# Feed-forward input projections by seven quarter products in place of eight, weights prepared from a work list, output projection in six stretches

## The chip, the cores and the metric

The kernel runs on 1 core of one Trainium2 chip. The metric is the device time of one execution in microseconds (us). Before the change the median of three runs is 1221.57 us (1219.39, 1221.57 and 1223.93). The profile comes from one execution of its own, which took 1222.08 us.

## The reference

The program computes one transformer block on 512 tokens of width 1024, in float32: a norm with modulation, one wide input projection, two attention-like branches (stick-breaking attention and retention), their output projections with gates, and then a gated feed-forward. The change touches the end of it, with `w_out` 1024x1024, `w_ffn_in` 1024x5632 and `w_ffn_out` 2816x1024:

```python
        merged = (g_sb * jnp.einsum('bse,ed->bsd', o_sb, w_proj_sb[l])
                  + g_ret * jnp.einsum('bse,ed->bsd', o_ret, w_proj_ret[l]))
        x = x + gate1[:, None, :] * jnp.einsum('bsd,de->bse', merged, w_out[l])

        hffn = modulate(rmsnorm(x, g_norm2[l]), shift2, scale2)
        a, u = jnp.split(jnp.einsum('bsd,df->bsf', hffn, w_ffn_in[l]), 2, axis=-1)
        x = x + gate2[:, None, :] * jnp.einsum('bsf,fd->bsd', jax.nn.silu(a) * u, w_ffn_out[l])

    return rmsnorm(x, g_final)
```

## The kernel before

**Numbers in two parts.** Activations are kept transposed, feature on the 128 partitions and the 512 tokens on the free axis. Every float32 operand is split in two: a high part, which ACT writes as a rounded copy (`fp32r`, L203), and a low part, which DVE writes as source minus high part (L205). A product of two such pairs is three matmuls (`mm3`): high by high, high by low, low by high. The low by low part is left out. `weight` loads one 128x1024 block of weights (512 KB, by a DMA that SP issues at L198 into one of three `raw` buffers), and splits it into one of three `whi` and three `wlo` buffers; `gemm` runs `mm3` over the blocks of the contraction. All matmuls of the kernel are issued at one line, L224.

**The stages from `w_out` on.** The output projection (`wo`) makes eight column blocks of 128. Each has 24 matmuls over all 512 tokens, and `residual`, one DVE operation that multiplies by the gate and adds to `x1`. `add_residual` treats the last three (NSPLIT) differently: it runs them over the first 256 tokens, then over the second, so that the norm of the first half (`half_rms`: column sums by small matmuls in a PSUM tile `z`, a reciprocal square root, a broadcast by small matmuls) is worked on beside the matmuls of the second. `norm2` then scales and splits 256 tokens of each of the eight activations (`xn`, L908 and L909, then L203 and L205) into `hf`, tiles of tag `q`.

The feed-forward has 22 column blocks of 128, each with a weight block for `a` and one for `u` (24 matmuls each, 512 wide, into PSUM tiles `ps`). `ff_act` then makes silu(a) times u: ACT's silu from PSUM (L917), DVE's product (L918), and a split. The blocks run in three chunks of 8, 8 and 6 (`FF_CHUNKS`). After each chunk its part of `w_ffn_out` is multiplied, eight output blocks, each added to `x1` at L951; the last chunk does this through `add_residual` again, followed by the final norm and the stores.

**The order.** The program is written in the order in which it should run, and the tile framework gives each instruction its place on its engine by that order and by when buffers come free; a tile of a tag waits for the last reader of the tile that had its buffer. Each engine takes its instructions in order and waits at semaphores. In the rows of orders further on, "waits Activation_49" is a wait for ACT, DVE_49 for DVE, PE_49 for PE, DMAHW for a transfer that SP issued, DMASW for one that POOL issued; numbers behind names tell buffers apart.

Of the kernel before, what the change touches and what calls it, by code (L numbers as in the profile page):

```python
# [11 lines left out]
F32 = mybir.dt.float32  # L12
# [7 lines left out]
P = 128  # L20
# [16 lines left out]

PE_SHIFT = (1, 2, 4)

FF_CHUNKS = ((0, 8), (8, 8), (16, 6))  # L40


def weight_plan():
# [38 lines left out]
    for i in range(NF):  # L82
        add(("fa", i), "w_ffn_in", 0, 8, rng(i * P, P))
        add(("fu", i), "w_ffn_in", 0, 8, rng(DFF + i * P, P))
    for c, (k0, nk) in enumerate(FF_CHUNKS):
        for i in range(8):
            add(("fo", c, i), "w_ffn_out", k0 * P, nk, rng(i * P, P))
# [25 lines left out]
def kernel(  # L113
# [20 lines left out]
    def nm(s):  # L134
        uid[0] += 1
        return f"{s}_{uid[0]}"
# [7 lines left out]
    def psz():  # L144
        return pspool.tile([P, S], F32, tag="z", bufs=BUFS["z"], name=nm("z"))

# [76 lines left out]
    def mm(o, lhs, rhs, start, stop):  # L223
        nc.tensor.matmul(o, lhs, rhs, start=start, stop=stop, skip_group_check=True)  # L224
# [6 lines left out]
    def gemm(o, w, acts, start=True, stop=True, t0=0, t1=S):  # L231

        hi, lo = w
        n = len(acts)
        for k in range(n):
            a = acts[k]
            mm3(o, hi[:, k, :], lo[:, k, :], a[:, 0, t0:t1], a[:, 1, t0:t1],
                start and k == 0, stop and k == n - 1)


# [612 lines left out]

    HALVES = (slice(0, 256), slice(256, 512))

    def half_rms(sq, half):
        o = psz()
        for b in range(2):
            c = half.start + b * P
            mm(o[:, b : b + 1], sq[:, c : c + P], ones[:, 0:1], b == 0, b == 1)  # L860
        v = small(4)[:, 0:2]
        nc.vector.tensor_scalar(v, o[:, 0:2], 1.0 / D, EPS, op0=ALU.mult, op1=ALU.add)
        y, cst = rsqrt_act(v)
        r = psz()
        for b in range(2):
            dg = cpool.tile([P, P], F32, tag="diag", bufs=3, name=nm("diag"))
            nc.vector.tensor_scalar(dg, ident, y[:, b : b + 1], cst, op0=ALU.mult, op1=ALU.mult)
            mm(r[:, b * P : (b + 1) * P], ones, dg, b == 0, b == 1)
        return r[:, 0:256]

    x1 = [None] * 8
    NSPLIT = 3

    def add_residual(get, gcol, acc, on_half):


        for d in range(8 - NSPLIT):
            o = ps()
            gemm(o, *get(d))
            nc.vector.scalar_tensor_tensor(  # L880
                x1[d], o, mod[:, gcol + d : gcol + d + 1], x1[d], op0=ALU.mult, op1=ALU.add
            )
            acc = sumsq(x1[d], acc)
        last = [(d, ps(), get(d)) for d in range(8 - NSPLIT, 8)]
        rs = []
        for hv in HALVES:
            for d, o, (w, acts) in last:
                gemm(o[:, hv], w, acts, t0=hv.start, t1=hv.stop)
                nc.vector.scalar_tensor_tensor(
                    x1[d][:, hv], o[:, hv], mod[:, gcol + d : gcol + d + 1], x1[d][:, hv],  # L890
                    op0=ALU.mult, op1=ALU.add,
                )
# [6 lines left out]
        x1[d] = otile()  # L899
        nc.sync.dma_start(x1[d], xT[d * P : (d + 1) * P, :])  # L900

    hf = [pair("q") for _ in range(8)]

    def norm2(n, hv, r):
        for j in range(8):
            a, sh = gains2[j]
            xn = apool.tile([P, 256], F32, tag="v", bufs=BUFS["v"], name=nm("xn"))
            nc.vector.tensor_mul(xn, x1[j][:, hv], r)  # L908
            nc.scalar.activation(xn, xn, AF.Identity, bias=sh, scale=a)  # L909
            split(hf[j][:, 0, hv], hf[j][:, 1, hv], xn)  # L910

    add_residual(lambda d: (weight(("wo", d)), ms), 16, None, norm2)


    def ff_act(a, u, tag):
        t = tmp()
        nc.scalar.activation(t, a, AF.Silu)  # L917
        nc.vector.tensor_mul(t, t, u)  # L918
        hl = pair(tag)
        split(hl[:, 0, :], hl[:, 1, :], t)  # L920
        return hl

    def final_norm(n, hv, r):
        for d in range(8):
# [3 lines left out]
            )  # L928
            nc.sync.dma_start(out[d * P : (d + 1) * P, hv], x1[d][:, hv])

    for c, (k0, nk) in enumerate(FF_CHUNKS):
        acts = []
        tag = "h" if c == 1 else "s"
        for i in range(k0, k0 + nk):
            a, u = ps(), ps()
            wa, wu = weight(("fa", i)), weight(("fu", i))
            if i == 0:
                for hv in HALVES:
                    for o, w in ((a, wa), (u, wu)):
                        gemm(o[:, hv], w, hf, t0=hv.start, t1=hv.stop)  # L940
            else:
                gemm(a, wa, hf)
                gemm(u, wu, hf)
            acts.append(ff_act(a, u, tag))
        if c == 2:
            ln_exp_tables()
        if c < 2:
            for d in range(8):
                o = ps()
                gemm(o, weight(("fo", c, d)), acts)  # L950
                nc.vector.scalar_tensor_tensor(  # L951
                    x1[d], o, mod[:, 40 + d : 41 + d], x1[d], op0=ALU.mult, op1=ALU.add
                )
        else:
            add_residual(lambda d: (weight(("fo", 2, d)), acts), 40, None, final_norm)


def host_constants():
# [63 lines left out]
```

## Time and the profile before

| | us | |
|---|---|---|
| median of three runs | 1221.57 | 1219.39 to 1223.93 |
| profiled execution | 1222.08 | its span, first to last instruction, is 1220.3 |
| PE (matmuls) | 1195.5 | 98% of the span, 5966 matmuls |
| PEld (weight loads, beside PE) | 1010.4 | 83% |
| DVE | 707.9 | 58% |
| ACT | 491.2 | 40% |
| POOL | 12.4 | 1% |
| from the first matmul of `wo` to the first of the feed-forward | 61.62 | 796.28 to 857.90 |
| the feed-forward, up to the last three output blocks' second half | 335.94 | 857.90 to 1193.84 |
| the last half outputs, and the final norm and stores | 14.44 and 12.02 | 1193.84 to 1220.30 |

The granted clock of PE over the execution is 0.997 of full speed. Busy times of matmuls are modelled at their ends and overlap, so the pace of a run of matmuls is read from starts and not from the mean of a group. In a row of a group of instructions stand the line, engine, operation, output and inputs by name, sizes, count, then busy time and the mean of one in ns, then the idle time before them and what ended it. In a row of the timeline the first number is the start and the second the length, both in us from the start of the span.

### The profile page before, as it was taken

How to read it: one execution, taken by the hardware profiler on the slowest of the kernel's cores; microseconds unless marked ns; L12 is line 12 of the kernel's file. 1: busy time of each engine (PE TensorE's matmuls, PEld its weight loads, DVE VectorE, ACT ScalarE, POOL GpSimd, SP SyncE). 2: the span in 40 equal slices, each digit the busy share in tenths (PEclk: the TensorE clock that was granted, in tenths of full speed). 3: DMA queues.
4: the chain of work that ended last, by engine and by line, in shares of the span. 5: the costliest groups of instructions: out<-in, count | busy, mean ns of one | idle time of the engine just before them, and what ended most of it. 6: DMA issues, size and time to landing. Idle time of an engine off the chain costs nothing.

```text
span 1220.3 us, 15168 instructions
## 1 busy us (share of the span) xinstructions
PE 1195.5 (98%) x5966; PEld 1010.4 (83%) x5966; DVE 707.9 (58%) x1139; ACT 491.2 (40%) x765; POOL 12.4 (1%) x36
## 2 busy tenths in 40 slices
PE   8999999999999999999999999999999999999996
PEld 6888778888888888898888888888888888888886
DVE  6888885645554543387878787547433333333335
ACT  5442323322332332376777677325432122322332
POOL 0010000000000000000000000000000000000000
PEclk9999999999999999999999999999999999999998
DMA  9746761231232264426362625332323233233222
GB/s 357 252 128 227 247 227 52 88 103 52 88 111 70 73 171 140 143 73 163 88 153 79 164 66 195 120 104 70 101 89 104 88 102 104 87 104 90 91 78 69
DMA packets 48233, 149.83 MB, mean 123 GB/s; under 512 B 6049, under 2 KB 8225, under 8 KB 48162
## 3 DMA queue, kind: packets, MB, share of 16 engines
q1 hardware_dynamic: 48162, 148.87, 39.1%
q8 instruction: 47, 0.77, 0.3%
q14 instruction: 24, 0.20, 0.1%
HBM read 129.97 MB, written 4.19 MB: 110 GB/s over the span
## 4 chain that ended last, share of the span: by engine, by line
PE 90%; DVE 5%; DMA 3%; ACT 1%; issue 1%; POOL 0%; SPq 0%; DVEq 0%; ACTq 0%
PE ps L224 76%; PE z L224 11%; PE av L224 3%; DMA araw<-wada 3%; DVE araw L251 1%; DVE wlo L205 0%; DVE t L271 0%; DMA o<-xT 0%; DVE o L925 0%; ACT xn L909 0%; DVE s L205 0%; DVE t L644 0%; POOL s L561 0%; DVE t L643 0%; DVE q L205 0%
## 5 line engine op out<-in xcount | busy, mean ns | idle before, releaser
L203 ACT ACTIVATE whi<-raw 128x1024 fp32r<-128x1024 f32 (+1 forms) x182 | 191.1, 1050 | 513.3 <-PE ps L224 415.9
L224 PE MATMUL ps<-h,whi 128*128 128x512 f32 (+1 forms) x1312 | 397.0, 383 | 0.1
L205 DVE TENSOR_TENSOR wlo<-raw,whi 128x1024 fp32r<-128x1024 f32 (+1 forms) x182 | 220.4, 1211 | 172.4 <-ACT whi L203 170.3
L224 PEld LDWEIGHTS ps<-h,whi 128*128 128x128 f32 x1312 | 241.1, 188 | 44.1
L224 PE MATMUL ps<-h,wlo 128*128 128x512 f32 (+1 forms) x656 | 248.3, 382 | 0.0
L224 PE MATMUL ps<-q,whi 128*128 128x512 f32 (+1 forms) x800 | 238.3, 381 | 0.4 <-ACT q L203 0.4
L224 PEld LDWEIGHTS ps<-q,whi 128*128 128x128 f32 x800 | 148.1, 188 | 29.0 <-ACT q L203 0.6
L224 PE MATMUL ps<-s,whi 128*128 128x512 f32 (+1 forms) x580 | 169.9, 376 | 1.5 <-DVE v L205 1.5
L224 PE MATMUL ps<-q,wlo 128*128 128x512 f32 (+1 forms) x400 | 152.3, 381 | 2.1 <-DVE wlo L205 2.1
L224 PEld LDWEIGHTS ps<-h,wlo 128*128 128x128 f32 x656 | 123.4, 188 | 23.2
L224 PEld LDWEIGHTS ps<-s,whi 128*128 128x128 f32 x580 | 106.6, 188 | 21.8 <-DVE v L205 1.9
L224 PE MATMUL ps<-whi,h 128*128 128x256 f32 (+1 forms) x480 | 115.4, 326 | 2.2 <-DVE t L642 2.2
L224 PE MATMUL ps<-s,wlo 128*128 128x512 f32 (+1 forms) x290 | 109.0, 376 | 0.0
L224 PEld LDWEIGHTS ps<-whi,h 128*128 128x128 f32 x480 | 82.3, 190 | 11.1 <-DVE t L642 3.1
L205 DVE TENSOR_TENSOR s<-t,s 128x512 fp32r<-128x512 f32 (+1 forms) x126 | 79.3, 651 | 18.0 <-ACT s L203 17.8
L224 PEld LDWEIGHTS ps<-q,wlo 128*128 128x128 f32 x400 | 75.2, 188 | 16.8 <-DVE wlo L205 2.3
L203 ACT ACTIVATE s<-t 128x512 fp32r<-128x512 f32 (+1 forms) x126 | 72.6, 599 | 26.9 <-DVE t L752 23.2
L224 PE MATMUL ps<-wlo,h 128*128 128x256 f32 (+1 forms) x240 | 78.0, 325 | 0.0
L224 PEld LDWEIGHTS ps<-s,wlo 128*128 128x128 f32 x290 | 54.6, 188 | 9.9
L918 DVE TENSOR_TENSOR t<-t,ps 128x512 f32<-128x512 f32 x22 | 15.1, 687 | 72.1 <-PE ps L224 71.4
L224 PEld LDWEIGHTS ps<-wlo,h 128*128 128x128 f32 x240 | 45.5, 190 | 4.0
L224 PE MATMUL z<-q,q 128*128 128x256 f32 (+2 forms) x224 | 44.6, 329 | 0.0
(154 smaller groups left out, 1104.9 us busy)
## 6 DMA issues: line engine op xcount, KB each, us to landing
raw<-wp SPq DMA_DIRECT2D x174, 512.0 KB, 3.5
araw<-wada SPq DMA_DIRECT2D x32, 512.0 KB, 4.4
sraw<-wada SPq DMA_DIRECT2D x16, 512.0 KB, 7.2
q<-qp SPq DMA_DIRECT2D x32, 256.0 KB, 3.6
raw<-wp SPq DMA_DIRECT2D x16, 384.0 KB, 3.6
o<-xT SPq DMA_DIRECT2D x16, 256.0 KB, 3.9
q<-qp SPq DMA_DIRECT2D x32, 128.0 KB, 3.1
spill<-t SPq DMA_DIRECT2D x8, 256.0 KB, 3.9
```

The source lines that it names most:

```text
L203: nc.scalar.activation(dst_hi, src, AF.Copy, scale=scale)
L205: (eng or nc.vector).tensor_sub(dst_lo, src, f(dst_hi))
L224: nc.tensor.matmul(o, lhs, rhs, start=start, stop=stop, skip_group_check=True)
L251: nc.vector.scalar_tensor_tensor(raw, raw, 1.0, cact, op0=ALU.mult, op1=ALU.mult, accum_out=col)
L918: nc.vector.tensor_mul(t, t, u)
```

## The change

**Seven products.** Strassen's scheme in Winograd's form. The 512 tokens are cut in two halves of 256, the 1024 of the contraction in two halves of 512, and the columns of one *pair* (two blocks of `a` with the two blocks of `u` that belong to them) in `a` and `u`, 256 columns each. A pair's product is then two by two quarters, which would take eight quarter products, and takes seven here on sums of quarters. A quarter product `(p, n)` is 24 matmuls (two column blocks, four contraction blocks, `mm3`), each 256 wide, into one 128x512 PSUM tile. There are 11 pairs. The weights in packed form are laid out by quarter (`("ff", p, half, c)`, 128x1024).

- On the side of the activations DVE makes the sums S1 to S4 once, in place of `hf` (`high7`, `low7`, tiles of 128x1024).
- On the side of the weights each pair has four loads (two through `raw`, two through `araw`), DVE sums t5, t6, t4 (`sums`) and t7 (`sum7`), and seven splits. For the four sums the split is as before, ACT high, DVE low. For the three plain quarters (n = 1, 2, 3) and for the blocks of `w_ffn_out` before the last stretch it is `split_dma`: ACT writes the high part and its negative, and a DMA issued by POOL adds the source onto the negative.
- The results are put together from PSUM by DVE adds (`u2`, `u3`, `p1`) beside silu and products.

**The order.** The items of the work list are the products of a pair in the order 1, 6, 5, 7, 2, 4, 3, with an output item (`("out", c, i)`, 256 columns of `w_ffn_out`) after the third and the sixth; `prepare_item` is called for the item five places ahead (`AHEAD`) of the product that runs. `w_ffn_out` now comes in six stretches of 1, 2, 2, 2, 2 and 2 pairs instead of three chunks. Pair 0's weights and a part of pair 1's are prepared during `wo`; the last four of the eight `wo` blocks run by half tokens, with the second norm and the first six products, in an order that is written out by hand (`manual_schedule`) for DVE, ACT and PE. The last stretch goes through `add_residual` as before.

**Buffers.** `whi` and `wlo` have four buffers instead of three; the tiles `table` and `cact`, used in earlier stages, take buffers of `wlo` and `whi` instead of their own.

```diff
-FF_CHUNKS = ((0, 8), (8, 8), (16, 6))
+FF_CHUNKS = ((0, 1), (1, 2), (3, 2), (5, 2), (7, 2), (9, 2))
...
-BUFS = dict(raw=3, araw=2, whi=3, wlo=3, h=8, q=8, v=4, s=8, qp=2, o=8, t=7, ps=4, z=3, av=1, sm=12)
+BUFS = dict(raw=3, araw=2, whi=4, wlo=4, h=8, q=8, v=4, s=8, qp=2, o=8, t=7, ps=4, z=3, av=1, sm=12)
...
-        t = cpool.tile([P, 2 * S], F32, tag="table", bufs=1, name=nm("table"))
+        t = wpool.tile([P, WCOLS], F32, tag="wlo", bufs=BUFS["wlo"], name=nm("table"))
...
-    cact = cpool.tile([P, D], F32, name="cact")
+    cact = wpool.tile([P, D], F32, tag="whi", bufs=BUFS["whi"], name="cact")
...
+    def split_dma(src, hi, lo):
+        nc.scalar.activation(hi, src, AF.Copy)
+        nc.scalar.activation(lo, f(hi), AF.Copy, scale=-1.0)
+        nc.gpsimd.dma_start(f(lo), src, accum_op=ALU.add)
+        return hi, lo
+
+    def high(t, hi):
+        nc.scalar.activation(hi, t, AF.Copy)
+        return hi
+
+    def low(t, hi, lo):
+        nc.vector.tensor_sub(lo, t, f(hi))
+        return hi, lo
...
+    def sums(p, tags):
+        raw = raws_of.setdefault(p, {})
+        for half, c, tag in ((0, 0, "raw"), (0, 1, "araw"), (1, 1, "araw"), (1, 0, "raw")):
+            if (half, c) not in raw:
+                raw[half, c] = load_ff(p, half, c, tag)
+        t = sums_of[p] = {n: raw_quarter(tag) for n, tag in zip((5, 6, 4), tags)}
+        nc.vector.tensor_sub(t[5], raw[0, 1], raw[0, 0])
+        nc.vector.tensor_sub(t[6], raw[1, 1], t[5])
+        nc.vector.tensor_sub(t[4], raw[1, 0], t[6])
...
+    def prepare(p, n, tags=None):
+
+        raw = raws_of.setdefault(p, {})
+        if n == 6 and p > 0:
+            sums(p, "ssh")
+        if n == 7:
+            sum7(p)
+        if n < 3:
+            if (n - 1, 0) not in raw:
+                raw[n - 1, 0] = load_ff(p, n - 1, 0, "raw")
+            w = split_dma(raw[n - 1, 0], *(wtile(t) for t in tags or " sh"[n] * 2))
+        elif n == 3:
+            w = split_dma(raw[1, 1], wtile("whi"), wtile("wlo"))
+        else:
+            t = sums_of[p][n]
+            w = low(t, high(t, wtile("whi")), wtile("wlo"))
+        ready[p, n] = w
+
+    SEVEN = {1: "A11", 2: "A12", 3: "S4", 4: "A22", 5: "S1", 6: "S2", 7: "S3"}
+    part = {}
+
+    def product(p, n, o, first, last, at=None, then=None, late=False):
...
+        for i in range(2):
+            c = slice(i * P, (i + 1) * P)
+            for k in range(4):
+                if i * 4 + k == at:
+                    then()
+                oc = o[:, i * 256 : (i + 1) * 256]
+                a, z = first and i == 0 and k == 0, last and i == 1 and k == 3
...
+                    mm3(oc, hi[:, k, c], lo[:, k, c], ah[:, k, :], al[:, k, :], a, z)
...
+    def run_product(p, n):
+
+        d = part.setdefault(p, {})
+        if n == 1:
+            d["x"] = psz()
+            product(p, 1, d["x"], True, False)
+            d["p1"] = tmp()
+            nc.scalar.activation(d["p1"], d["x"], AF.Copy)
+        elif n == 2:
+            product(p, 2, d["x"], False, True)
+            d["s0"] = tmp()
+            nc.scalar.activation(d["s0"], d["x"], AF.Silu)
+        elif n == 6:
+            d["z"] = psz()
+            product(p, 6, d["z"], True, False)
+            d["u2"] = tmp()
+            nc.vector.tensor_add(d["u2"], d["z"], d["p1"])
...
+        elif n == 7:
+            product(p, 7, d["z"], False, False)
+            d["u3"] = tmp()
+            nc.vector.tensor_add(d["u3"], d["z"], d["p1"])
+            nc.vector.tensor_add(d["u3"], d["v"], d["u3"])
+        elif n == 4:
+            product(p, 4, d["z"], False, True)
+            nc.vector.tensor_add(d["p1"], d["z"], d["p1"])
+            nc.scalar.activation(d["p1"], d["p1"], AF.Silu)
...
+            for hv, t in zip(HALVES, (d["u2"], d["u3"])):
+                split(hi[:, :, hv], lo[:, :, hv], t.rearrange("p (a b) -> p a b", a=2))
...
+    def prepare_out(c, i):
+        ready["out", c, i] = out_weight(c, i, split_dma)
+
+    def run_out(c, i):
+        for j, w in enumerate(ready.pop(("out", c, i))):
+            o = ps()
+            gemm(o, w, ff_acts[c])
+            residual(2 * i + j, o, 40)
...
+    NP, NC, AHEAD = NF // 2, len(FF_CHUNKS), 5
...
+    FIRST = [(0, 1), (0, 2), (1, 1), (0, 4), (1, 2), (0, 6), (0, 5), (0, 7)]
...
+            for n_, m in enumerate((1, 6, 5, 7, 2, 4, 3)):
+                if (p, m) not in FIRST:
+                    work.append((p, m))
+                    if n_ in (2, 5) and len(outs) > (1 if c == NC - 1 else 0):
+                        work.append(outs.pop(0))
+        work += outs
+        outs = [("out", c, i) for i in range(4)]
+    for m in (2, 1):
+        work.remove((2, m))
+        work.insert(1, (2, m))
...
+    with tc.manual_schedule(engines={nc.vector.engine, nc.scalar.engine, nc.tensor.engine}):
...
+        product(0, 1, d0["x"], True, True, 7, lambda: c1.append(half_colsum(acc, h1)))
...
+        g1 = half_scale(
+            c1[0], lambda: nc.vector.tensor_sub(l01[:, S:], m01[:, S:], f(a01)[:, S:])
+        )
...
+        product(0, 2, d0["x2"], True, True, 4, lambda: r1.append(half_bcast(g1)))
+        m11, m10 = raw_quarter("h"), raw_quarter("h")
+        scaled(m11, 1, range(4), h1, r1[0])
+        high7("A22", m11, "q")
+        scaled(m10, 0, range(4), h1, r1[0])
+        sum7(0)
+        low7("A22", m11, "q")
+        k7, k5 = high(t0[7], wtile("h")), high(t0[5], wtile("whi"))
+        s1, s2, s3, s4 = m11, raw_quarter("h"), m10, m01
+        nc.vector.tensor_add(s1, m10, m11)
+        nc.vector.tensor_sub(s2, s1, m00)
+        high7("S2", s2, "qp")
+        nc.vector.tensor_sub(s4, m01, s2)
+        ready[0, 5] = low(t0[5], k5, wtile("h"))
+        low7("S2", s2, "q")
+        product(1, 1, d1["x"], True, True)
...
+        product(0, 4, d0["y"], True, True, late=True)
+        d1["x2"] = ps()
+        product(1, 2, d1["x2"], True, True)
+        d0["z"], d0["v"] = psz(), psz()
+        product(0, 6, d0["z"], True, False, late=True)
+        high7("S1", s1, "qp")
+        nc.vector.tensor_sub(s3, m00, s3)
+        low7("S1", s1, "q")
+        high7("S3", s3, "q")
+        ready[0, 7] = low(t0[7], k7, wtile("h"))
+        low7("S3", s3, "q")
...
+        high7("S4", s4, "q")
+        product(0, 5, d0["v"], True, False, late=True)
+        product(0, 7, d0["z"], False, True, late=True)
+        low7("S4", s4, "q")
...
+    for it in work:
+        while queue and work.index(queue[0]) <= work.index(it) + AHEAD:
+            prepare_item(queue.pop(0))
+        (run_out if it[0] == "out" else run_product)(*it[-2:])
...
+    add_residual(last_out, 40, final_norm, 3)
```

**On PE, around the second column block of the feed-forward.** Before, a block of `a` (`ps_7578`) is 24 matmuls 512 wide on `q` tiles, the halves of the normed activation, and waits once for ACT's high part and once for DVE's low part of its weights:

```order
L224 MATMUL ps_7578<-q_6970,whi_7587 128x512 [waits Activation_49]
L224 MATMUL ps_7578<-q_6970,whi_7587 128x512
L224 MATMUL ps_7578<-q_6970,wlo_7588 128x512 [waits DVE_49]
L224 MATMUL ps_7578<-q_6971,whi_7587 128x512 x2
L224 MATMUL ps_7578<-q_6971,wlo_7588 128x512
```

Now, at the end of product (1,6) in `z_7893`, then (1,5) in `z_7925`, in which the beginning of (2,2) in `z_7829` stands, whose high and low weights are `h_7774` and `h_7775`:

```order
L225 MATMUL z_7893<-qp_7561,whi_7768 128x256
L225 MATMUL z_7893<-q_7566,whi_7768 128x256
L225 MATMUL z_7893<-qp_7561,wlo_7770 128x256
L225 MATMUL z_7925<-qp_7669,whi_7779 128x256 [waits DVE_49]
L225 MATMUL z_7925<-q_7672,whi_7779 128x256
L225 MATMUL z_7829<-v_7415,h_7775 128x256 [waits DMASW6_49]
L225 MATMUL z_7829<-v_7415,h_7774 128x256
L225 MATMUL z_7829<-v_7445,h_7774 128x256
```

A wait for a transfer that POOL issued stands on PE now, where no wait for a transfer stood.

**On ACT, beside the same place.** Before, the high parts of the weights (`whi`) alternate with the silu out of PSUM (`t<-ps`) and the high part of its product (`s`):

```order
L917 ACTIVATE t_7571<-ps_7461 128x512 [waits PE_49]
L203 ACTIVATE whi_7649<-raw_7647 128x1024 [waits DMAHW3_49,PE_49]
L203 ACTIVATE s_7574<-t_7571 128x512 [waits DVE_49]
L203 ACTIVATE whi_7655<-raw_7653 128x1024 [waits DMAHW4_49,PE_49]
L917 ACTIVATE t_7639<-ps_7577 128x512 [waits PE_49]
```

Now stand there the high parts of (1,6) and (1,5), the high part and its negative for (2,2) (`h_7774`, `h_7775`), the copy of (2,1)'s result out of PSUM, and the two steps of an output item (`whi_7785`, `wlo_7786`):

```order
L960 ACTIVATE whi_7768<-s_7763 128x1024 [waits DVE_49]
L1273 ACTIVATE t_7499<-t_7499 128x512 [waits DVE_49]
L960 ACTIVATE whi_7779<-s_7762 128x1024 [waits PE_49]
L954 ACTIVATE h_7774<-raw_7772 128x1024 [waits DMAHW0_49,Activation_49]
L1042 ACTIVATE t_7854<-z_7829 128x512 [waits PE_49]
L955 ACTIVATE h_7775<-h_7774 128x1024 [waits Activation_49]
L954 ACTIVATE whi_7785<-raw_7783 128x512 [waits DMAHW1_49]
L204 ACTIVATE s_7817<-t_7746 128x2x256 [waits DVE_49]
L955 ACTIVATE wlo_7786<-whi_7785 128x512 [waits DMASW3_49,Activation_49]
```

ACT has a second pass over the plain quarters and output blocks now, and waits in order at each of PE, DVE and the transfers.

**On SP, which issues the loads.** Before, each load waits for the transfer that used its queue slot and for DVE's last reading of its buffer:

```order
L198 DMA raw_7919<-wp 128x1024 [waits DMAHW0_49,DVE_49]
L198 DMA raw_7925<-wp 128x1024 [waits DMAHW1_49,DVE_49]
L198 DMA raw_7987<-wp 128x1024 [waits DMAHW2_49,DVE_49]
L198 DMA raw_7993<-wp 128x1024 [waits DMAHW3_49,DVE_49]
L198 DMA raw_8054<-wp 128x1024 [waits DMAHW4_49,DVE_49]
```

Now, at pair 2 and the loads behind it (`araw_7952` is quarter (1,1) of pair 2, whose buffer was last read by the adding DMA of item (1,3), DMASW1):

```order
L199 DMA raw_8103<-wp 128x512 [waits DMAHW3_49,DMASW0_49,Activation_49]
L972 DMA araw_7952<-wp 128x1024 [waits DMAHW7_49,DMASW1_49,Activation_49]
L972 DMA raw_8167<-wp 128x1024 [waits DMAHW0_49,DMASW6_49,DVE_49]
L972 DMA araw_8190<-wp 128x1024 [waits DMAHW2_49,DVE_49]
L972 DMA raw_8194<-wp 128x1024 [waits DMAHW4_49,DMASW2_49,Activation_49]
L199 DMA raw_8263<-wp 128x1024 [waits DMASW3_49,DMAHW7_49,DVE_49,Activation_49]
```

A load that refills a buffer of a plain quarter or of an output block now waits for a transfer of POOL's, and the loads behind it on SP wait with it.

More of the change, by code (lines that the diff above doesn't have):

```diff
@@ L900 @@
         nc.sync.dma_start(x1[d], xT[d * P : (d + 1) * P, :])
[L902 to L912, printed above, removed]
@@ new lines, in out_weight @@
+    def out_weight(c, i, lo_by):
+        idx = WIDX["fo", c, i]
+        nk = PLAN[idx][3]
+        n = nk * 256
+        raw = load_raw(wp[idx], n)[:, :n]
+        hi, lo = wtile("whi")[:, :n], wtile("wlo")[:, :n]
+        lo_by(raw, hi, lo)
+        return [
+            tuple(t.rearrange("p (k c) -> p k c", k=nk)[:, :, j * P : (j + 1) * P] for t in (hi, lo))
+            for j in range(2)
+        ]
+    def prepare_out(c, i):
[5 more added lines that the diff above has]
+            residual(2 * i + j, o, 40)
@@ new lines, with prepare_item @@
+    for m in (2, 1):
+        work.remove((2, m))
+        work.insert(1, (2, m))
+    def prepare_item(it):
+        (prepare_out if it[0] == "out" else prepare)(*it[-2:])
+    acc = None
+    for d in range(4):
+        o = ps()
+        gemm(o, weight(("wo", d)), ms)
+        residual(d, o, 16)
+        acc = sumsq(x1[d], acc)
+        if d == 0:
+            prepare(0, 1, "qq")
+        elif d == 1:
+            prepare(0, 2, "qq")
+        elif d == 2:
+            sums(0, "sss")
+            t0 = sums_of[0]
+            ready[0, 4] = low(t0[4], high(t0[4], wtile("s")), wtile("s"))
+            k6 = high(t0[6], wtile("s"))
+        else:
+            prepare(1, 1, "qq")
+            ready[0, 6] = low(t0[6], k6, wtile("s"))
@@ new lines @@
+    queue = list(work)
+    queue.remove((1, 6))
+    queue.insert(2, (1, 6))
+    prepare_item(queue.pop(0))
+    for d in (d0, d1):
+        d["s0"] = tmp()
+        nc.vector.tensor_add(d["s0"], d["x2"], d["p1"])
+        nc.scalar.activation(d["s0"], d["s0"], AF.Silu)
+    d0["u3"] = tmp()
+    nc.vector.tensor_add(d0["u3"], d0["z"], d0["p1"])
+    nc.vector.tensor_add(d0["p1"], d0["y"], d0["u3"])
+    nc.scalar.activation(d0["p1"], d0["p1"], AF.Silu)
+    nc.vector.tensor_add(d0["u3"], d0["v"], d0["u3"])
```

226 lines of the change are left out of this document (171 added, 55 removed).

## The prediction

> **What bounds the kernel now.** I read the page from the top: span, busy shares, the chain that ended last. Then the stretch that the change rewrites, from the first matmul of the `wo` projection (796.28 us) to the end, by windows; then the order of time inside it.
>
> ```profile
> span 1220.3 us, 15168 instructions
> PE 90%; DVE 5%; DMA 3%; ACT 1%; issue 1%; POOL 0%; SPq 0%; DVEq 0%; ACTq 0%
> 796.28:857.90 61.62, 58.92 (x374) 53.28 (x373) 37.23 (x77) 28.52 (x57) 0.00 (x0) 1.00 0.25 80
> 857.90:1193.84 335.94, 335.94 (x1487) 278.41 (x1487) 121.41 (x131) 94.37 (x114) 0.00 (x0) 1.00 0.30 94
> 1193.84:1208.28 14.44, 14.44 (x117) 13.91 (x115) 9.52 (x24) 3.97 (x9) 0.00 (x0) 1.00 0.05 16
> 1208.28:1220.30 12.02, 1.77 (x8) 1.42 (x8) 6.33 (x19) 0.82 (x3) 0.00 (x0) 0.67 0.47 157
> ACT whi L203 <- PE ps L224: 198.2, 54, 4.4
> ```
>
> The columns of a window are its length, then busy time of PE, PEld, DVE, ACT and POOL, the granted TensorE clock and DMA. In the feed-forward (857.90 to 1193.84) PE is busy all the time at the full clock, DVE 36% and ACT 28%, and ACT waits for PE to free weight buffers, never the reverse. So the price of this stretch is the number of matmuls times their pace. The pace, from the first and last start of an unbroken run of each width:
>
> ```profile
> 900.08 0.62 PE L224 MATMUL ps<-q,whi 128*128 128x512 f32 x2
> 918.44 0.62 PE L224 MATMUL ps<-q,whi 128*128 128x512 f32 x2
> 837.22 0.40 PE L224 MATMUL ps<-h,whi 128*128 128x256 f32 x2
> 841.89 0.40 PE L224 MATMUL ps<-h,whi 128*128 128x256 f32 x2
> 844.80 0.39 PE L224 MATMUL ps<-q,wlo 128*128 128x256 f32 x1 [2.14 <-DVE wlo L205]
> ```
>
> Each row of these stands at the head of a group of three matmuls. 512 wide: 27 groups, 81 matmuls in 18.36 us, 226.7 ns each. 256 wide: 13 groups, 39 in 4.67 us, 119.7 ns. Two narrow ones cost 239.4, 5.6% more than a wide one: halving the columns does not halve the time, and the change doubles the number of matmuls before it saves an eighth of the work.
>
> **Matmul time.** Before, from `wo` on: 512 wide 120 (`wo`) + 1008 + 384 + 90 = 1602, and 256 wide 144 + 96 + 108 = 348; 1602 x 0.2267 + 348 x 0.1197 = 404.8 us. With the tail of 12.0 that leaves 424.0 - 416.8 = 7.2 us of waits and small matmuls, about 1.5 in the last half tokens, 5.7 around the second norm. After: 512 wide 96 + 432 + 60 = 588; 256 wide 192 + 11 pairs x 7 products x 24 = 1848 + 72 = 2112; 133.3 + 252.8 = 386.1. **Saved: 18.7 us.** The Trainium skill ("TensorE: Matmul & The Clock Gate", section "Back-to-back issue gap") gives N/2.4 + 2.5 ns warm, so 215.8 and 109.2 ns; by it the saving would be 26.2 us and the forecast 7.5 lower. The trace is 10.5 to 10.9 ns a matmul above it at both widths, and the measured pace is what I use.
>
> **Feeding in the steady stretch.** Prices of the new steps, from the same forms in the trace:
>
> ```profile
> L203 ACT ACTIVATE whi<-raw 128x1024 fp32r<-128x1024 f32 x174 | 184.3, 1060 | 490.4 <-PE ps L224 402.1 <-issue 83.8 <-PE z L224 4.0
> L205 DVE TENSOR_TENSOR wlo<-raw,whi 128x1024 fp32r<-128x1024 f32 x174 | 212.7, 1223 | 168.5 <-ACT whi L203 166.4
> L918 DVE TENSOR_TENSOR t<-t,ps 128x512 f32<-128x512 f32 x22 | 15.1, 687 | 72.1 <-PE ps L224 71.4 <-ACT t L917 0.7
> L951 DVE SCALAR_TENSOR_TENSOR o<-ps,mod,o 128x512 f32<-128x512 f32 x16 | 12.0, 750 | 52.1 <-PE ps L224 52.1
> L203 ACT ACTIVATE s<-t 128x512 fp32r<-128x512 f32 x94 | 58.2, 628 | 26.1 <-DVE t L752 23.2 <-DVE t L590 2.0
> L917 ACT ACTIVATE t<-ps 128x512 f32<-128x512 f32 x22 | 12.8, 582 | 0.0
> 850.13 1.41 DVE L908 TENSOR_TENSOR xn<-o,z 128x256 f32<-128x256 f32 x4 [0.67 <-PE z L224]
> ```
>
> Two pairs and a chunk's output take PE 336 x 0.1197 + 96 x 0.2267 = 62.0 us. ACT: 28 copies of 128x1024 (ten a pair, eight for the outputs) x 1.06 and ten of 128x512 x 0.63 = 36.0. DVE: 16 sums and low parts x 1.22, 18 adds, products and splits x 0.69 and 8 residuals x 0.75 = 37.9. Both fit, and cost nothing as long as the order gives them lead. If that cover went, PE would wait for whole steps of 1.1 to 1.2 us.
>
> **The price that no row shows.** `split_dma` takes the low part off DVE: ACT writes -hi, and a DMA issued by POOL adds the source to it. The trace has no DMA from POOL and none that adds. Call its time, from the end of -hi to the landing, L. The nearest rows:
>
> ```profile
> raw<-wp SPq DMA_DIRECT2D x174, 512.0 KB, 3.5
> sraw<-wada SPq DMA_DIRECT2D x16, 512.0 KB, 7.2
> q<-qp SPq DMA_DIRECT2D x32, 256.0 KB, 3.6
> q<-qp SPq DMA_DIRECT2D x32, 128.0 KB, 3.1
> GB/s 357 252 128 227 247 227 52 88 103 52 88 111 70 73 171 140 143 73 163 88 153 79 164 66 195 120 104 70 101 89 104 88 102 104 87 104 90 91 78 69
> ```
>
> Low end 3.5 (one 512 KB load); high end 7.2 (the same size in the crowded first slices). I take 5.0: 3.5 plus reading the destination as well, 512 KB at the 357 GB/s of the busiest slice, 1.5 us. A reason for a longer one, two reads and a write in turn at 3.5 each, gives 10.5. The Trainium skill ("DMA: Bandwidth & Descriptors", section "Anatomy of one DMA") has 2.0 us + bytes/436e3 for a DMA from POOL, 3.2 us here; by it alone the forecast would be 1204.9. No run here shows that yet.
>
> **Where L lies on PE's path.** Every wait below is PE's, and all PE work stands behind it; meanwhile ACT, in order, waits for PE's weight slots.
>
> - *Norm and pair 0*, without L. The two half norms: 0.8 of waits, 1.6 of small matmuls, 0.15 for the high part of S2. Then `(1,6)`: from the second norm broadcast DVE has 8 scales (1.41 for four, above), 13 steps of 1.22, an add, two adds, another add (4 x 0.69) and the sum t6 of pair 1 (1.22), with 0.7 of hand-overs 23.4; its high part on ACT 1.06, so 24.5. PE has 180 narrow matmuls, 21.7. Wait 2.8. Sum 5.35.
> - *(2,2)*: ACT goes on with a silu (0.63), two high parts, a copy out of PSUM (0.58) and -hi, done at 28.9, landed at 28.9 + L; PE is there after 52 more matmuls, at 30.8. Wait L - 1.9.
> - *second output of chunk 0*: slot freed, hi and -hi of 128x512 (2 x 0.63), 0.15, then L, against 24 narrow and 14 wide matmuls, 6.05. Wait L - 4.65.
> - *(2,6)*, by the `araw` buffer: slot freed, hi, -hi (2.12), L, only then the next load (3.5), sum t6 (1.22), hi (1.06): L + 7.9, against 72 narrow and 12 wide, 11.3; and 0.75 for its low part. Wait L - 2.65. Behind that load on SP stand those of pairs 2 and 3.
> - *(3,6)*, the same loop with 96 narrow and 12 wide (14.4): wait L - 5.1.
> - *pairs 3 to 10*: the same loop with 120 narrow and 24 wide, 20.0, against L + 10.0 with DVE's other steps. Nothing up to L = 10, then 8 times the excess.
>
> At L = 5: 5.35 + 3.1 + 0.35 + 2.35 = 11.15 us, where before had 5.7.
>
> **Elsewhere, nothing.** Pair 0's weights are made in `wo`: eight copies on ACT (8.5 us) in eight rounds of 5.44, in which the stage used 1.7 each. The sharing of tiles moves one load on SP, the mask's, behind the fourth spill store; it is used first at 516.08:
>
> ```profile
> 496.57 0.81 SPq L807 DMA_DIRECT2D spill<-t x1
> 516.08 0.90 DVE L583 TENSOR_TENSOR z<-z,table 128x512 f32<-128x512 f32 x2 [3.22 <-PE z L224]
> table<-consts SPq DMA_DIRECT2D x1, 256.0 KB, 3.9
> ```
>
> Landing by 501, it has 15 us in hand. The tail has the same steps behind its last matmul, 12.0 us. Its halves are 36 matmuls instead of 54, with the chain of the first half still in them: 1.5 of waits again.
>
> **Sum**, against the profiled execution (1222.08 us: span 1220.3 and 1.8 around it): 1222.1 - 18.7 - 5.7 + 11.15 = 1208.9, say **1209.0**. The median of the three runs shown is 0.5 lower, inside their spread of 4.5.
>
> **Rivals.**
>
> - *Accumulation a little slower than I take it*, L 6.8 to 9.9: the four waits grow by up to 4 us for each us of L. At 7.2, 19.85 of waits, 1217.6; no gain at all at 8.3. For: 512 KB took 7.2 when the queues were full. Against: DMA is 0.30 busy here.
> - *The buffer loop becomes the bound, slower than before.* Place: `araw` of item 3, whose next load waits for the accumulation, ahead of the sums. From L = 9.9 the kernel is slower by over 0.5%; at 10.5, 37.05 us of waits, 1234.8; at 12, 1252.8. For: three transfers in turn are 10.5, and POOL must build them. Against: the 128 and 256 KB rows above (`q<-qp`) are at 3.1 and 3.6 us, so a small transfer costs most of its time once, not three times.
> - *A narrow matmul at half of a wide one*, 113.4 ns, if the fixed part is hidden in long unbroken runs: 2112 x 6.3 ns = 13.4 us less, 1195.6. Against: the 39 above are such a run. The skill's gap, named above, lies on this side.
>
> **How the numbers follow.** No change is within 0.5%, 6.1 us, about what a measurement can tell. Faster by more needs waits under 18.3, L under 6.8; slower by more, L over 9.9. My case (L 3.2 to 6.8, 1204.8 to 1216.0): 0.59. Half price: 0.04. Between: 0.17. Loop: 0.20. So faster 0.63, same 0.17, slower 0.20. The range leaves out the half price and the loop beyond three transfers in turn (L over 10.5, 1234.8): 1203 to 1235, about 0.16 left out; the likeliest case alone is 1205 to 1216.
>
> **What would show it.** Right: narrow products at 119 to 121 ns and a stretch from `wo` of 411 us; POOL's accumulating rows 4 to 6 us to landing; PE waits of 2 to 3 us at `z` of (1,6), (2,2) and (2,6) and none after pair 3; clock 1.00. Wrong: DMA named as releaser of `z` matmuls in the later pairs (L over 10); DVE or ACT named there (order, not L); a clock under 1.00 behind the early waits; or a different pace.

## The result and the profile after

The changed kernel takes 1259.97 us (median of four runs, 1258.51 to 1263.32) against 1222.75 us before in the same session. The ratio is 1.031, with a 95% interval of 1.028 to 1.034: slower by 37 us, where 1209 was forecast and 1235 was the far end of the range. The profiled execution has a span of 1256.8 us, against 1220.3.

The page of the kernel after: span, busy shares, PE's clock and the DMA engines in 40 slices, and the chain that ended last.

```profile
span 1256.8 us, 17044 instructions
PE 1195.8 (95%) x6716; PEld 1042.2 (83%) x6716; DVE 793.4 (63%) x1242; ACT 582.6 (46%) x854; POOL 57.2 (5%) x89
PEclk9999999999999999999999999899989999999998
DMA  9656762322331374335535346613567666676552
PE 60%; DMA 19%; issue 9%; DVE 8%; ACT 3%; POOL 0%; SPq 0%; POOLq 0%; DVEq 0%; ACTq 0%
```

PE was 90% of the chain before and is 60% now, with DMA at 19%. The last 15 slices are the rewritten part: the DMA engines, 0.2 to 0.3 busy there before, are 0.5 to 0.7 busy in most of them, and the clock has gaps.

The table of waits of PE in the kernel after, from the first matmul of `wo` (799.03 us) to the end: who waited for whom, total us, times, longest.

```profile
PE ps L225 <- DMA wlo<-raw: 14.4, 8, 3.2
PE z L225 <- DVE t L1068: 7.2, 7, 1.4
PE ps L225 <- ACT h L204: 5.5, 1, 5.5
PE z L225 <- ACT whi L960: 3.4, 3, 2.0
PE z L225 <- DVE wlo L964: 2.5, 4, 1.2
PE z L225 <- DMA h<-raw: 2.1, 1, 2.1
```

With two waits of the final norm (2.4 and 1.8, where before had 1.7 and 1.7) and two single ones of 0.9 and 0.7 these are 40.9 us; the same stretch before had 6.0. From the starts of the matmuls in the traces, the stretch from the first matmul of `wo` to the last matmul divides so (us):

| | before | after | difference |
|---|---|---|---|
| wide x 0.2267 + narrow x 0.1197, and the small ones | 406.8 | 388.1 | -18.7 |
| waits of PE | 6.0 | 40.9 | +34.9 |
| slower pace at half clock | 0.3 | 11.8 | +11.5 |
| the rest (ramps behind waits, changes of width) | 3.7 | 9.7 | +6.0 |
| sum | 416.8 | 450.5 | +33.7 |

The stretch also begins 2.75 us later than before (799.03 against 796.28); the 7 us behind the last matmul are the same. So the products did save what was forecast, and waits and the clock took it back almost three times over.

The counts and the pace came out as worked out: 588 wide and 2112 narrow matmuls. In the timeline of PE after, the first and the last row of a run of narrow ones:

```profile
938.72 0.28 PE L225 MATMUL z<-q,wlo 128*128 128x256 f32 x1
949.88 0.28 PE L225 MATMUL z<-qp,wlo 128*128 128x256 f32 x1
```

These are 93 matmuls in 11.16 us, 120.0 ns each, against 119.7 before.

The DMA issues of the kernel after (output and input, queue, count, size, median us from issue to landing):

```profile
raw<-wp SPq DMA_DIRECT2D x156, 512.0 KB, 3.9
wlo<-raw POOLq DMA_DIRECT2D x17, 512.0 KB, 5.3
wlo<-araw POOLq DMA_DIRECT2D x11, 512.0 KB, 7.8
s<-raw POOLq DMA_DIRECT2D x9, 512.0 KB, 5.2
h<-raw POOLq DMA_DIRECT2D x9, 512.0 KB, 5.9
```

With three into `q` and four of 256 KB there are 53 adding DMAs. From the end of ACT's pass to the issue are 0.3 us, so that L, taken as 5.0, is 5.5 at the median of the 26 that were issued with no other adding DMA under way (plain loads can stand beside them). The 27 others took 7.5 at the median and up to 10.0. They come in groups: in the timeline of POOL and SP between pairs 7 and 8,

```profile
1097.88 0.86 POOL L956 DMA_DIRECT2D s<-raw  x1 [4.06 <-ACT s L955]
1099.91 0.86 POOL L956 DMA_DIRECT2D wlo<-raw  x1 [1.17 <-ACT wlo L955]
1101.95 0.86 POOL L956 DMA_DIRECT2D wlo<-araw  x1 [1.18 <-ACT wlo L955]
1103.53 4.01 SPq L199 DMA_DIRECT2D raw<-wp  x2
1110.88 11.64 SPq L972 DMA_DIRECT2D araw<-wp  x2
```

three adding DMAs are issued 2.04 us apart and land at 1103.39, 1107.16 and 1110.83, 3.7 us apart (2.5 to 4.7 in the other groups of three between 990 and 1185 us); SP issues the next loads at 1103.53, 1107.21 and 1110.88, each right behind a landing. The chain of waits goes through these (start, length, what):

```profile
1097.88 5.52 DMA s<-raw
...
1103.53 7.49 DMA raw<-wp
...
1111.09 9.49 issue
...
1120.60 5.25 DMA wlo<-raw
...
1125.89 5.52 DMA raw<-wp
```

Behind the "issue" of 9.49 stands work that the chain does not name. POOL waits there for ACT, and ACT, in its order, for the sum of the next pair. The load for that sum goes into an `araw` buffer, and SP could issue it only at 1110.88, when the third adding DMA had landed. In the timelines of DVE and ACT:

```profile
1114.47 1.23 DVE L982 TENSOR_TENSOR s<-araw,s 128x1024 f32<-128x1024 f32 x1 [7.50 <-DMA araw<-wp]
1115.73 2.01 ACT L960 ACTIVATE whi<-s 128x1024 fp32r<-128x1024 f32 x2 [8.09 <-DVE s L982]
1131.44 1.06 ACT L954 ACTIVATE s<-raw 128x1024 fp32r<-128x1024 f32 x1 [5.85 <-DMA raw<-wp]
```

So one ring goes through both kinds of buffers: the third adding DMA of a group (8.9 us), the load into `araw` (3.6), the sum and ACT's passes up to the next adding DMA (6.2), this one (5.2), a load into the `raw` buffer that it leaves (5.6), and ACT's passes up to the third adding DMA of the next group, issued at 1137.96 (6.5). That is 36.0 us for one pair, and PE stands nowhere in it. Between the third adding DMAs from 964.67 us to 1174.55 a pair takes 33.4 to 36.6 us. PE has 7 x 24 x 0.1199 + 48 x 0.2267 = 31.0 us of matmuls in a pair, so it has to wait.

### The profile page after: what moved, and what is told of

The parts are those of the page before. It is cut to its first block, busy times and chain, and to the rows that moved or that the text cites. A ratio compares the mean times of both kernels' runs of the same rounds, so it can differ in the third digit from the quotient of the medians.

```text
span 1256.8 us, 17044 instructions
## 1 busy us (share of the span) xinstructions
PE 1195.8 (95%) x6716; PEld 1042.2 (83%) x6716; DVE 793.4 (63%) x1242; ACT 582.6 (46%) x854; POOL 57.2 (5%) x89
## 3 DMA queue, kind: packets, MB, share of 16 engines
q0 software_dynamic: 7632, 26.74, 11.8%
## 4 chain that ended last, share of the span: by engine, by line
PE 60%; DMA 19%; issue 9%; DVE 8%; ACT 3%; POOL 0%; SPq 0%; POOLq 0%; DVEq 0%; ACTq 0%
PE ps L225 45%; PE z L225 12%; DMA raw<-wp 7%; PE av L225 3%; DMA wlo<-raw 3%; DMA wlo<-araw 2%; DMA araw<-wada 2%; DMA s<-raw 2%; DMA araw<-wp 1%; DVE araw L253 1%; DMA q<-raw 1%; DMA t<-t 1%; DVE wlo L964 1%; DVE o L1101 0%; DVE wlo L206 0%
## 5 line engine op out<-in xcount | busy, mean ns | idle before, releaser
L225 PE MATMUL ps<-h,whi 128*128 128x512 f32 (+1 forms) x1416 | 422.2, 380 | 5.5 <-ACT h L204 5.5
L204 ACT ACTIVATE whi<-raw 128x1024 fp32r<-128x1024 f32 x118 | 124.9, 1059 | 260.1 <-PE ps L225 226.5
L206 DVE TENSOR_TENSOR wlo<-raw,whi 128x1024 fp32r<-128x1024 f32 x118 | 143.9, 1220 | 86.8 <-ACT whi L204 50.0
L225 PE MATMUL ps<-s,whi 128*128 128x512 f32 x480 | 150.2, 394 | 1.7 <-DVE v L206 1.7
L225 PE MATMUL z<-q,whi 128*128 128x256 f32 x664 | 139.2, 287 | 0.7 <-DVE t L1274 0.7
L225 PEld LDWEIGHTS z<-q,whi 128*128 128x128 f32 x664 | 112.2, 195 | 2.7 <-DVE t L1274 0.9
L225 PE MATMUL ps<-s,wlo 128*128 128x512 f32 x240 | 95.4, 398 | 9.0 <-DMA wlo<-raw 9.0
L225 PE MATMUL z<-q,wlo 128*128 128x256 f32 x248 | 71.0, 286 | 0.0
L891 DVE SCALAR_TENSOR_TENSOR o<-ps,mod,o 128x512 f32<-128x512 f32 (+1 forms) x63 | 42.3, 687 | 38.3 <-PE ps L225 38.1
L225 PE MATMUL z<-qp,whi 128*128 128x256 f32 x168 | 48.7, 292 | 10.6 <-DVE t L1068 7.2
L960 ACT ACTIVATE whi<-s 128x1024 fp32r<-128x1024 f32 x21 | 21.2, 1051 | 71.9 <-DVE s L982 71.9
```

The costliest lines, as they stand in the source:

```text
L204: nc.scalar.activation(dst_hi, src, AF.Copy, scale=scale)
L206: (eng or nc.vector).tensor_sub(dst_lo, src, f(dst_hi))
L891: nc.vector.scalar_tensor_tensor(x1[d][:, hv], o[:, hv], mod[:, gcol + d : gcol + d + 1], x1[d][:, hv], op0=ALU.mult, op1=ALU.add,)
L960: nc.scalar.activation(hi, t, AF.Copy)
```

## The experiments

All were compared with the kernel before in their own session. The times of the stretch are from the first matmul of `wo` to the last matmul, its parts as in the table above; they come from the one profiled execution of each kernel, the times and ratios from all executions.

| kernel | us | ratio to before (95%) | stretch | waits | half clock |
|---|---|---|---|---|---|
| before | | | 416.8 | 6.0 | 0.3 |
| the change | 1259.97 | 1.0312 (1.0281 to 1.0344) | 450.5 | 40.9 | 11.8 |
| all low parts by DVE | 1215.70 | 0.9959 (0.9936 to 0.9982) | 408.6 | 11.6 | 3.7 |
| output blocks by DVE | 1240.13 | 1.0163 (1.0110 to 1.0217) | 432.8 | 28.6 | 8.6 |
| item 3 by DVE | 1252.15 | 1.0232 (1.0187 to 1.0276) | 441.1 | 36.2 | 7.8 |
| first three blocks by DVE | 1255.91 | 1.0277 (1.0237 to 1.0318) | 448.3 | 40.1 | 9.5 |
| a quarter of the bytes | 1218.27 | 0.9966 (0.9945 to 0.9987) | 410.0 | 11.3 | 3.5 |
| order by hand in `wo` | 1256.81 | 1.0279 (1.0232 to 1.0325) | 445.7 | 38.2 | 8.9 |
| order by hand, all by DVE | 1212.31 | 0.9900 (0.9865 to 0.9935) | 405.2 | 9.8 | 1.9 |

**All low parts by DVE.**

```diff
     def split_dma(src, hi, lo):
         nc.scalar.activation(hi, src, AF.Copy)
-        nc.scalar.activation(lo, f(hi), AF.Copy, scale=-1.0)
-        nc.gpsimd.dma_start(f(lo), src, accum_op=ALU.add)
+        nc.vector.tensor_sub(lo, src, f(hi))
         return hi, lo
```

and the same for the block of item (1,2) in the part ordered by hand. (There are 53 such blocks; the 54 below counts one too many.)

> The low parts of all 54 weight blocks that the adding DMA made come from DVE again (ACT's second pass goes with it). Theory 1, the adding transfers: three are issued within 4 us, share one path, and the loads of the next pair stand behind their landing. Then the waits of PE from the output projection on fall from 40.9 us to 5 to 12, the half-clock stretches behind them go (11.8 us), and the time is 1208 to 1220. Theory 2, the order: what waits is ACT and DVE in their order (the waits named DVE t, DVE wlo and ACT whi, some 15 us, and the 5.5 us in the output projection), and DVE gets 54 x 1.22 = 65 us more. Then waits stay over 25 us and the time is 1235 to 1255.

Measured 1215.70, with 11.6 us of waits. Theory 1 stands, theory 2 falls: the waits that were named after DVE and ACT went together with those named after DMA, although DVE got more to do. The waits of PE that were left, from `wo` on:

```profile
PE z L225 <- DVE diag L874: 2.4, 1, 2.4
PE ps L225 <- ACT h L204: 2.3, 1, 2.3
PE z L225 <- DVE t L273: 1.8, 1, 1.8
PE z L225 <- ACT whi L959: 1.6, 1, 1.6
PE z L225 <- DVE q L940: 1.3, 1, 1.3
...
```

The rest are under 0.8 each, and none lies between 924 and 1205 us, in the steady pairs: with DVE as the maker the cover of that stretch holds, as the prediction had counted it.

**A quarter of the bytes.**

```diff
-        nc.gpsimd.dma_start(f(lo), src, accum_op=ALU.add)
+        q = src.shape[1] // 4
+        nc.gpsimd.dma_start(f(lo)[:, 0:q], src[:, 0:q], accum_op=ALU.add)
```

> Each adding DMA moves only the first quarter of its block (128 KB instead of 512 KB), the rest of the low part is left as minus the high part: same instructions, same waits, a quarter of the bytes. Theory 1, in which the bytes of the transfers queue behind each other: from the end of ACT's second pass to landing 3 to 3.5 us for all three of a group instead of 5, 7 and 8.5, and the time 1216 to 1230. Rival, in which the fixed part of a POOL DMA and the chain of waits through it cost, not its bytes: L stays over 4.5 in the groups and the time over 1245.

Measured 1218.27. With the same instructions, second passes and waits for landings, the waits fell to 11.3 us. The DMA issues of this kernel:

```profile
wlo<-raw POOLq DMA_DIRECT2D x17, 128.0 KB, 2.9
wlo<-araw POOLq DMA_DIRECT2D x11, 128.0 KB, 4.5
s<-raw POOLq DMA_DIRECT2D x9, 128.0 KB, 2.7
```

So L went from 5.5 alone and 7.5 behind others to 3.0 and 4.3; the 3 to 3.5 expected for all of a group was too low for those behind another, and the 4.5 of `wlo<-araw` is where the rival had put L. But the time is theory 1's: it is the time that the bytes take, and not POOL's issuing or the number of waits, that made the kernel slow. (Three quarters of each low part are left out here, so this kernel is a measurement and not a version to use.)

**Output blocks by DVE.** `prepare_out` splits with `split` in place of `split_dma`; 33 adding DMAs stay.

> DVE makes the low part of the 20 output blocks only; the 33 quarter products keep the adding DMA. Theory 1: groups of three become groups of two, the third landing comes 3.6 us earlier, the 14.4 us of waits for wlo of output blocks go and most half-clock stretches with them: 1232 to 1244. Theory 2: the waits for DVE grow by what the waits for DMA lose: 1250 to 1260.

Measured 1240.13, in the range of theory 1. Waits for `wlo<-raw` are gone. The part of the ring that goes through `araw` is left: a row of waits of PE reads

```profile
PE z L225 <- DMA h<-raw: 6.7, 3, 3.9
```

and in the chain of waits stand, one behind the other,

```profile
1089.50 9.45 DMA wlo<-araw
...
1099.00 3.48 DMA araw<-wp
```

**Item 3 by DVE**, the third of each group, and the one the prediction's second rival named.

```diff
-            w = split_dma(raw[1, 1], wtile("whi"), wtile("wlo"))
+            w = low(raw[1, 1], high(raw[1, 1], wtile("whi")), wtile("wlo"))
```

> Only the low part of item 3 (the 11 quarters in araw) comes from DVE, so that the araw buffer is free without an adding DMA; the other 42 keep it. If the araw loop is what bounds the pairs, as the prediction's rival has it, the waits of the steady pairs go nearly all: 1228 to 1236. If it is the group of three as a whole (each adds 3.6 us to the ones behind it), a group of two is left, as when the output blocks are taken out: 1236 to 1246. If neither, 1252 or more.

Measured 1252.15: neither 1228 to 1236 nor 1236 to 1246, and at the edge of the range for neither. The `araw` loop alone was not the bound. Waits of PE for output blocks stay as they were:

```profile
PE ps L225 <- DMA wlo<-raw: 14.9, 9, 4.2
```

Four loads a pair go through the three `raw` buffers (two plain quarters and two output blocks), and they still wait for adding DMAs. The load into `araw` waits for none now, but SP issues it in order behind two of those. In the timelines of SP and ACT:

```profile
1064.31 3.20 SPq L199 DMA_DIRECT2D raw<-wp  x2
1067.61 0.37 SPq L972 DMA_DIRECT2D araw<-wp  x1
1074.30 2.01 ACT L960 ACTIVATE whi<-s 128x1024 fp32r<-128x1024 f32 x2 [9.95 <-DVE s L982]
```

The second load of the first row was issued at 1067.18, when an adding DMA had landed at 1067.11, and ACT still waited 9.95 us for the sum. In the stretch, taking the output blocks out of the ring brought 17.7 us, item 3 alone 9.4, and everything together 41.9. The other two plain quarters were not taken out by themselves. Whether a fourth `raw` buffer, or another order of the loads on SP, would loosen the ring was not tried.

**First three blocks by DVE**, those prepared in `wo`, and **order by hand in `wo`**. In the change ACT's order in `wo` is (timeline of ACT, selected rows)

```profile
806.69 1.06 ACT L954 ACTIVATE q<-raw 128x1024 fp32r<-128x1024 f32 x1 [5.12 <-DMA raw<-wp]
807.78 1.06 ACT L955 ACTIVATE q<-q 128x1024 fp32r<-128x1024 f32 x1
808.74 0.61 ACT L204 ACTIVATE h<-t 128x512 fp32r<-128x512 f32 x1
```

that is, the high part of the last merged activation (`h`), for which PE stood 5.46 us, lies behind two passes for pair 0. The chain of waits shows what these waited for:

```profile
798.51 4.56 DMA q<-raw
803.09 3.58 DMA raw<-wp
```

an adding DMA had to leave a `raw` buffer before their load could start. The first kernel makes only these three low parts on DVE.

> DVE makes the low part of the three blocks that are prepared during the output projection; the rest keeps the adding DMA. Theory 1: ACT's copies of pair 0 no longer stand behind a raw buffer that an adding DMA holds, so the 5.46 us wait on the last high part of the merged activations and its 6.83 us at half clock (3.4 us) go: 1250 to 1254. Theory 2: ACT reaches those copies ahead of the activation's high part whatever makes the low part, and waits for the raw loads: 1257 to 1262.

Measured 1255.91, between the two. The wait fell from 5.46 to 1.81 and 0.57 us, so the adding DMA was most of it. All waits together fell only from 40.9 to 40.1, because later ones grew: 3.20 at (2,6), where the change had 2.01 and 0.45. The gain that theory 1 counted for the clock was also too high: in the change PE still waits during 2.9 of the 6.83 us at half clock, and the matmuls in the rest lose some 1.9, not 3.4. The second kernel writes the first four blocks out by hand, with the last high parts first and the weights two blocks ahead:

```diff
-    for d in range(4):
-        o = ps()
-        gemm(o, weight(("wo", d)), ms)
-        residual(d, o, 16)
...
+    ws = {d: weight(("wo", d)) for d in range(2)}
+    with tc.manual_schedule(engines={nc.vector.engine, nc.scalar.engine}):
+        for d in range(4):
+            o = ps()
+            gemm(o, ws[d], ms)
+            ws[d + 2] = weight(("wo", d + 2))
+            residual(d, o, 16)
...
-    wts = {d: weight(("wo", d)) for d in tail}
+    wts = {d: ws[d] if d in ws else weight(("wo", d)) for d in tail}
```

> The adding DMA everywhere, as in the change; only the order by hand in the first four blocks of the output projection. Theory 1: the 5.46 us wait and the 6.83 us at half clock in the output projection go, the rest stays: 1259 - 5.5 - 3.4 = about 1251. Rival (that wait comes from the adding DMA holding a raw buffer): it reappears in the next blocks, 1256 or more.

Measured 1256.81, the rival's range. The wait on `h` is gone, but 2.50 and 0.76 us stand 17 us later, on the weights of the sixth block:

```profile
PE ps L225 <- ACT whi L204: 2.5, 1, 2.5
```

**Order by hand and all low parts by DVE together.**

> All low parts by DVE, and besides that the first four blocks of the output projection are written out by hand for ACT and DVE, with each block's weights taken two blocks ahead, so that the preparation of pair 0 stands behind the last high parts of the merged activations. Theory 1 (what is left in this place is ACT's order): the waits of 2.26 and 0.57 us there and the 3.41 us at half clock behind them go, 2.8 + 1.7 = 4.5 us, and the time is 3 to 6 us below the kernel with DVE alone, 1209 to 1213, faster than before by 0.7 to 1%. Rival (the raw buffers are late whatever ACT's order): the wait moves to a later block or to the first products, and the time is that of the kernel with DVE alone.

Measured 1212.31, a ratio of 0.990 (0.9865 to 0.9935) to before: the fastest version here. The stretch is 405.2, 3.4 below DVE alone and 11.6 below before, of the 18.7 that the seven products save in matmuls. The wait on `h` is gone; 0.57 and 0.75 us stand at the sixth block. With nothing that waits for an adding DMA the change is worth 1%.

**Stalls by measure.** The kernel before, with ACT repeating one high part at seven places:

```diff
+        for _ in range(STALL.get(key, 0)):
+            nc.scalar.activation(hi[:, :n], raw[:, :n], AF.Copy)
         split(hi[:, :n], lo[:, :n], raw[:, :n], eng=eng)
```

with 9, 10, 11, 12, 13, 14 and 16 repeats in `fa` blocks 3, 5, 9, 11, 13, 15 and 18.

> The kernel before, with ACT repeating the high part of seven weight blocks 9 to 16 times (same data), so that PE is made to wait at seven places by growing amounts, from nothing to some 6 us. If PE's clock falls when it was idle for more than half of one 3.41 us period of a fixed grid, then waits under 1.7 us are followed by the full clock always, waits over 5.1 us by half clock always, and those between by where they fall; each such period costs up to 1.7 us besides the wait. Rival: the half clock has nothing to do with PE's waits (transfers, or load on the chip): no half-clock periods here.

Measured 1285.30 in one execution. PE waited 2.92, 4.32, 4.52, 6.19, 7.27, 8.36 and 10.54 us, more than meant, so that none of these seven was short enough to test the lower bound. With them the clock fell to half for 3.41, 3.41, 6.83, 6.83, 6.83, 10.24 and 10.24 us, behind the longer ones in part while PE still waited. Windows of one period each (length, busy PE, PEld, DVE, ACT, POOL, clock, DMA share and GB/s), two about the first stall, and one of each kernel about a wait for DVE that no repeat makes:

```profile
881.20:884.61 3.41, 0.51 (x2) 0.47 (x3) 1.91 (x3) 2.85 (x4) 0.00 (x0) 1.00 0.00 0
884.61:888.02 3.41, 3.41 (x9) 2.67 (x9) 2.97 (x3) 0.00 (x0) 0.00 (x0) 0.50 0.45 137
840.25:843.66 3.41, 1.27 (x11) 1.06 (x10) 3.41 (x8) 3.41 (x9) 0.00 (x0) 1.00 0.01 2
840.27:843.69 3.42, 2.38 (x20) 2.18 (x19) 3.35 (x11) 3.42 (x10) 0.00 (x0) 1.00 0.00 0
```

The last two rows are of the kernel with the stalls and of the kernel before. Both have the same wait of 2.14 us here. With the stalls it lies in one period, 2.14 us of it idle, and 6.83 us at half clock follow (why two periods, with PE busy in both, is open); before, an end of a period cuts it in two, 1.04 us are idle in this period and 1.11 in the next, and the clock stays full. So a wait of one length is followed by either clock, by where it falls in the periods, as expected for those between 1.7 and 5.1 us.

The stretch grew by 64.9 us, 44.1 of it the stalls and 20.0 the slower pace behind them. The rival falls: the half clock comes from PE's own idle time, with no transfer under way in the first of these windows.

## Why the prediction was wrong

- **Matmul time: right.** -18.7 us, to the tenth, and the narrow pace within 0.3 ns, so that the rival of half a wide one's price falls. Three PE times of the waits are a little above their own products (180 narrow ones are 21.5 us and not 21.7; 14.2 and not 14.4; 19.8 and not 20.0), which changes nothing.
- **L alone: nearly right.** 5.5 against 5.0, with 3.6 (one of 256 KB) to 8.9 as the ends of the lone ones. By the fit in the Trainium skill ("DMA: Bandwidth & Descriptors", section "Anatomy of one DMA") it would be an estimated 3.2; the trace disagrees for a DMA that adds.
- **One L for all: wrong.** The price of a lone transfer was used for transfers that come three in 4 us, and in such a group they land 2.5 to 4.7 us apart. SP's loads beside them are late as well: in the chain above they take 5.52 and 7.49, where the sum used 3.5.
- **The early waits** came out in part: (2,6) 2.46 against 2.35, (2,2) 2.13 against 3.1, none at (3,6), around (1,6) 0.89 and 0.74 against 2.8. The second output of chunk 0 did not wait (0.35 forecast): its block is 256 KB, and L was 3.6. The fourth, which was not priced, waited 2.86: its adding DMA was issued 0.6 us behind another one and took 6.8.
- **"Pairs 3 to 10: nothing up to L = 10": the step that failed.** It followed the `araw` loop by itself, from the moment at which PE frees a buffer for item 3, and held L + 10.0 against PE's 20.0. L of item 3 was 6.0 to 9.2 in pairs 3 to 9, under that limit, and still PE waited 21.2 us from 950 us up to the final norm, 3.2 at most at one place. What the runs show in its place: ACT comes to item 3 only behind its own wait for a `raw` load, which waited for an adding DMA in turn, so that `araw` and `raw` make one ring, of 33.4 to 36.6 us a pair against PE's 31.0. With a quarter of the bytes, or with DVE as the maker, PE's waits up to the final norm fall to 0.15 and 0 us from 950 us on. The second rival had the sign, the kind (a buffer loop in which the next load waits for the accumulation) and one half of the ring, but not the `raw` half, and so too high an L from which it decides.
- **"Elsewhere, nothing": wrong** in two places. In `wo` the eight copies were held against ACT's busy time, not against what they wait for in its order: 5.46 us, and some 1.9 for the matmuls at half clock behind it. And the stretch starts 2.75 us late: near 180 us PE waits 2.02 where it waited 0.43, with one period at half clock behind it. Most of the variants show that too (1.7 to 3.1 us of wait there, 0.64 in one); which of the moved buffers it comes from was not tested.
- **The clock: named as a sign, not priced.** It cost 11.5 us, a third of the waits again.

## What to carry to other kernels

Price a transfer that has taken an engine's work by what is under way when it is issued, not by its time alone, and follow every ring of buffers whose next load waits for it, turn by turn, also from one kind of buffer to another where an engine or a queue in order joins them. An engine in order waits for its slowest operand, so that copies with free time on the engine can still be late or make others late. And where PE is the bound, add to a wait of over half a clock period the slower matmuls behind it.

## What the runs showed of the hardware

**Adding transfers.** A DMA from POOL that adds 512 KB within SBUF takes 5.2 us from issue to landing by the median of `s<-raw`, 128 KB 2.7, and three issued 2.04 us apart 5.5, 7.3 and 8.9.

**The clock.** In these traces PE's clock changes only on a fixed grid of 3.41 us: in the kernel after, the stretches at half clock inside the program are 3.41 or 6.83 us long, and the one at full clock between the first two is 621.23, which is 182 x 3.4133. In that kernel, three periods in a row (columns as above):

```profile
949.90:953.31 3.41, 0.73 (x5) 0.29 (x3) 1.12 (x2) 2.49 (x3) 1.46 (x2) 1.00 0.94 185
953.31:956.72 3.41, 2.89 (x7) 2.31 (x8) 0.00 (x0) 0.00 (x0) 0.26 (x1) 0.50 1.03 191
956.72:960.13 3.41, 3.41 (x17) 2.79 (x16) 0.75 (x1) 0.00 (x0) 0.00 (x0) 1.00 1.00 280
```

Over all periods at full clock in the ten traces, idle time up to 1.71 us in a period was followed by the full clock with two exceptions (1.53, in the first period of the kernel with output blocks by DVE, and 1.69, at the end of the kernel with the stalls), and idle time of 1.88 us or more by half clock always; between, both occur. Half a period is 1.71. The Trainium skill ("TensorE: Matmul & The Clock Gate", Part 1, "What's actually happening") gives the period, and half rate after at least one idle window. The trace agrees on the period; here a window that is idle for just over half is enough: a wait of 2.13 us at one place, and two waits of 2.01 and 0.45 together at another.

**The start.** The full clock set in at 10.3 to 33.1 us in these executions, and `wo` began at 797.6 to 804.1 us in kernels that do the same until there, so that the stretch, and not the span, was compared above.
